# A diffusion layer on one core: the late modulation vectors as row sums on VectorE instead of products over partitions

## The chip, the cores and the metric

One core of one Trainium2 chip runs the whole kernel. The metric is device time in microseconds of one execution; the median of three timed runs of the kernel before is 1482.44 us (1481.68 to 1483.52). Engines are named TensorE (PE in the rows), VectorE (DVE), ScalarE (ACT) and GpSimd (POOL); transfers are issued from the queues of SyncE (SP) and GpSimd.

## The reference, cut to what matters

One layer of a diffusion backbone runs on 256 tokens and a context of 256 tokens, all in fp32. Six modulation vectors of 2048 features come from one product of the silu of the condition vector with a 2048 x 12288 matrix; everything else is large matrix products, a state space mixer (S5), a convolution and an attention of four heads.

```python
def _adaln(c_vec, w_mod, b_mod):
    m = jax.nn.silu(c_vec) @ w_mod + b_mod
    return jnp.split(m[..., None, :], 6, axis=-1)
...
sh1_x, sc1_x, g1_x, sh2_x, sc2_x, g2_x = _adaln(c, w_mod[l], b_mod[l])
...
hx = _rmsnorm(x, norm1_g[l]) * (1.0 + sc1_x) + sh1_x
zx = hx @ w_in[l] + b_in[l]
...
x = x + g1_x * (jnp.concatenate([s5_x, cv_x, ml_x], axis=-1) @ w_out[l])
hx2 = _rmsnorm(x, norm2_g[l]) * (1.0 + sc2_x) + sh2_x
x = x + g2_x * _swiglu(hx2, w_ffn_in[l], w_ffn_out[l])
```

The first two vectors (shift and scale of the first norm) are needed at the start. The other four, here called the late modulations and numbered q = 0 to 3 (g1, sh2, sc2, g2), are needed from the output projection on: q = 0 there, q = 1 and 2 at the second norm, q = 3 where the feed-forward output is added.

## The kernel before, in words

Features lie on partitions and tokens along the row. Every large weight matrix is cut into 128 x 128 tiles; they stream in one fixed order, eight tiles (512 KB) to a weight group, 386 groups in all. For each group SyncE loads `raw`, ScalarE casts it to `whi` (L201), and VectorE forms the rest `wlo = raw - whi` (L168). Each tile is then used by three matmuls (`mm3`): high x high, high x low, low x high. `raw`, `whi` and `wlo` have three buffers each, so VectorE can be ahead of TensorE by no more than that. The groups of the stages are: 0 to 13 phase 1, 14 to 29 the convolution's columns, 30 to 39 keys, 40 to 55 values, 56 to 71 queries, 72 to 87 the output gate o, 88 and 89 the S5 gate (glu), 90 to 121 the output projection in two halves, 122 to 385 the feed-forward.

Beside this main stream run side jobs, which are generators: the S5 mixer (16 pairs, each a chain between VectorE, ScalarE and TensorE), the convolution, the gates, the four attention heads, and the late modulations (`mod_job`). The class `Sched` keeps rough costs of the engines; at each weight group `pump` lets ready jobs emit steps, by priority, as long as the costs of VectorE and ScalarE are not too far ahead of TensorE. `need_mod(q)` forces the job on where a late modulation must be there. After that the compiler's list order fixes the sequence on every engine, and at run time each engine works through its own sequence.

A late modulation is a 2048 x 2048 product with a vector. It is taken in four blocks b of 512 output features. Weights come in slabs of 128 x 1024 (512 KB, tile `wm`, four buffers, issued from GpSimd's queue, L331); a slab holds 2 row tiles of 512 output features. Input features lie on partitions. For q = 0 (the set `MOD_PE`) TensorE multiplies: 16 native fp32 matmuls of 128x512 per block, four at a time on the 32-column strips of the array (L208, `ps_b<-wm,cs`). For q = 1 to 3 VectorE accumulates `macc = w * s + macc`, 15 instructions of 128x512 per block after one on ScalarE; each reads the result of the one in front. In both cases the sum over partitions is still to be taken: TensorE transposes `macc` (L749, four per block), and ScalarE sums the rows with an accumulating activation (L755), or VectorE reduces. `GO_AT` and `phase` hold q = 1 and 2 back until the keys, and q = 3 until the feed-forward has begun.

Of the kernel before, what the change touches and what calls it, by code (L numbers as in the profile page):

```python
# [19 lines left out]
KT = 16  # L20
# [14 lines left out]
MOD_PACE = 3200.0  # L35
MOD_PACE_F = 4000.0
MOD_PACE_D = 5000.0
# [6 lines left out]
GO_AT = {'k': 2}  # L44
LEAD_R, LEAD_S = 2, 1
MOD_PE = {(0, b) for b in range(4)}


# [58 lines left out]
class Sched:  # L107
    """Emits the tensor engine's main work in order and slips steps of side jobs in between."""
# [42 lines left out]
def hybrid_layer_kernel(ctx: ExitStack, tc: tile.TileContext, xt, ctxt, wm1, wmr, wst, wg, bvrow, pvd, cstd, s5p, out):  # L151
# [197 lines left out]
    # the order of the loads that share the queue up to the end of phase 1: by when they are needed  # L349
# [20 lines left out]
    cs = sb.tile([128, KT, 32], F32, name="cs")  # L370
# [3 lines left out]
    b1sc = sb.tile([128, 16], F32, name="b1sc")  # L374
# [66 lines left out]
    def s5_params():  # L441
# [43 lines left out]
        # half-angle sine and cosine  # L485
# [17 lines left out]
        # lambda_bar - 1 and its quotient by lambda  # L503
# [15 lines left out]
        # powers of lambda_bar  # L519
# [126 lines left out]
    def fourA(n, src, ps):  # L646
        """column tiles in turn, each over all rows: x tokens only"""
# [9 lines left out]
    def conv_job():  # L657
# [14 lines left out]
        def sum4(x):  # L672
            """sums over partitions and the four tiles, every partition the same"""
# [36 lines left out]
    def phase(n):  # L710
        mst["go"] = max(mst["go"], GO_AT.get(n, 0))

# [6 lines left out]
    def mod_job():  # L719
      for q in range(4):  # L720
        while mst["go"] < q:
            yield 500
        for b in range(4):
            on_pe = (q, b) in MOD_PE
            acc = sb.tile([128, 512], F32, name="macc", tag="macc", bufs=1)
            if on_pe:
                psm = bbank()
            for kp in range(0, 8, 2):
                w = [wm.pop((q, b, kp + i)).rearrange("p (k n) -> p k n", k=2) for i in range(2)]
                for j in range(4):  # L730
                    kt = 2 * kp + j
                    wj = w[j // 2][:, j % 2, :]
                    s = cs[:, kt, 0:1]
                    if on_pe:
# [675 lines left out]
```

## Time and profile before

| | |
|---|---|
| median of 3 timed runs | 1482.44 us |
| span of the profiled execution | 1479.6 us |
| TensorE busy | 1437.5 us, 97% |
| TensorE weight loads busy | 1351.2 us, 91% |
| VectorE busy | 1005.1 us, 68% |
| ScalarE busy | 716.0 us, 48% |
| DMA | 315.56 MB, 213 GB/s in the mean |

The profiled execution is not one of the three timed ones. Its span, from the first to the last instruction, is 2.84 us under their median; those 2.84 us are taken as what lies around the span. Busy shares of a whole span mix stages. In the slices of 37 us VectorE stands at 8 or 9 tenths busy from 160 to 440 us and at 4 or 5 tenths in the last third. A busy TensorE is modelled from pipelined matmuls, so a slice at 9 tenths can still hold short waits. The granted TensorE clock is 0.989 of full speed in the mean.

### The profile page before, as it was taken

The page shows a single profiled execution, that of the slowest core. Times are in us where ns is not written, and L with a number is a line of the kernel's source. Part 1 is how long each engine was busy: PE and PEld are TensorE (multiplying, and loading weights), DVE is VectorE, ACT ScalarE, POOL GpSimd, SP SyncE. Part 2 cuts the span into 40 slices and gives each one's busy share as a digit, 9 for nine tenths or more (in the row PEclk, how much of TensorE's full clock was granted, in tenths as well). Part 3 has the DMA queues.
Part 4 walks back from the last instruction along what each step waited for, and adds up shares of the span by engine and source line. Part 5 has one row for each costly group of instructions (what it writes and reads, how often), then busy time and mean ns, then how long its engine had stood idle before and what let it go on. Part 6 is the DMA issues. An engine that isn't in the chain of part 4 may idle for free.

```text
span 1479.6 us, 29243 instructions
## 1 busy us (share of the span) xinstructions
PE 1437.5 (97%) x11840; PEld 1351.2 (91%) x11840; DVE 1005.1 (68%) x1960; ACT 716.0 (48%) x1199; POOL 107.2 (7%) x207
## 2 busy tenths in 40 slices
PE   5999899999999999999899999999999999999996
PEld 3888788887888999999899999999999999999996
DVE  7555699988978887888776677455454554455554
ACT  4334776653565555645544444433444334443353
POOL 1221111110101110011000010000000000000000
PEclk9999999999999999999999999999999999999998
DMA  9997464442526666789477787555565555555553
GB/s 360 368 354 291 160 219 136 162 163 86 169 88 228 214 217 227 268 304 353 143 234 265 282 299 239 183 185 186 183 185 185 188 189 181 188 185 186 185 177 114
DMA packets 87943, 315.56 MB, mean 213 GB/s; under 512 B 10096, under 2 KB 10880, under 8 KB 87808
## 3 DMA queue, kind: packets, MB, share of 16 engines
q1 hardware_dynamic: 60912, 216.67, 44.1%
q0 software_dynamic: 26896, 97.02, 18.4%
q8 instruction: 93, 1.52, 0.4%
q14 instruction: 42, 0.34, 0.1%
HBM read 311.55 MB, written 2.10 MB: 212 GB/s over the span
## 4 chain that ended last, share of the span: by engine, by line
PE 89%; DVE 5%; ACT 3%; DMA 1%; issue 1%; SPq 0%; DVEq 0%; ACTq 0%
PE ps_m L208 70%; PE ps_b L208 13%; PE ps_qk L208 5%; DVE tmp L168 1%; DMA tmp<-in_wg_dram 1%; ACT tmp L195 0%; DMA raw<-in_wst_dram 0%; PE ps_b L839 0%; ACT whi L201 0%; ACT U L201 0%; DVE wlo L168 0%; DMA xr<-in_xt_dram 0%; ACT gT L201 0%; PE ps_b L749 0%; DVE tmp L191 0%
## 5 line engine op out<-in xcount | busy, mean ns | idle before, releaser
L168 DVE TENSOR_TENSOR wlo<-raw,whi 128x1024 fp32r<-128x1024 f32 x386 | 471.6, 1223 | 317.7 <-ACT whi L201 309.5
L201 ACT CAST whi<-raw 128x1024 fp32r<-128x1024 f32 x386 | 404.0, 1047 | 508.6 <-PE ps_m L208 373.8
L208 PE MATMUL ps_m<-h,whi 128*128 128x256 f32 x2624 | 470.4, 282 | 3.6 <-ACT h L195 3.6
L208 PEld LDWEIGHTS ps_m<-h,whi 128*128 128x128 f32 x2624 | 404.1, 189 | 4.0 <-ACT h L195 4.0
L208 PE MATMUL ps_m<-h,wlo 128*128 128x256 f32 x1312 | 370.0, 282 | 0.0
L208 PE MATMUL ps_m<-ffa,whi 128*128 128x256 f32 x1408 | 251.0, 281 | 0.0
L208 PEld LDWEIGHTS ps_m<-h,wlo 128*128 128x128 f32 x1312 | 247.8, 189 | 0.0
L208 PEld LDWEIGHTS ps_m<-ffa,whi 128*128 128x128 f32 x1408 | 215.7, 188 | 1.4 <-issue 1.2
L208 PE MATMUL ps_m<-ffa,wlo 128*128 128x256 f32 x704 | 197.2, 280 | 0.0
L208 PE MATMUL ps_m<-hx,whi 128*128 128x256 f32 x960 | 186.8, 290 | 5.5 <-ACT hx L195 3.6
L208 PEld LDWEIGHTS ps_m<-hx,whi 128*128 128x128 f32 x960 | 148.8, 190 | 24.8 <-issue 16.3
L179 DVE SCALAR_TENSOR_TENSOR macc<-wm,cs,macc 128x512 f32<-128x512 f32 x180 | 134.3, 746 | 6.6 <-ACT macc L195 5.1
L208 PE MATMUL ps_m<-hx,wlo 128*128 128x256 f32 x480 | 135.9, 284 | 0.0
L208 PEld LDWEIGHTS ps_m<-ffa,wlo 128*128 128x128 f32 x704 | 132.2, 188 | 0.0
L331 POOL DMA_DIRECT2D wm<-in_wmr_dram x128 | 67.5, 528 | 614.6 <-DVE macc L179 432.9
L208 PEld LDWEIGHTS ps_m<-hx,wlo 128*128 128x128 f32 x480 | 90.9, 190 | 0.2 <-DVE wlo L168 0.2
L179 DVE SCALAR_TENSOR_TENSOR xres<-ps_m,mods,xres 128x256 f32<-128x256 f32 x96 | 46.1, 481 | 35.0 <-PE ps_m L208 34.8
L179 DVE SCALAR_TENSOR_TENSOR XB<-XB,pv 128x256 f32<-128x256 f32 x120 | 53.7, 479 | 0.6
L208 PE MATMUL ps_m<-hc,whi 128*128 128x256 f32 x256 | 52.0, 284 | 0.0
L208 PE MATMUL ps_m<-mixm,whi 128*128 128x256 f32 x256 | 47.3, 286 | 0.0
L208 PE MATMUL ps_m<-whi,hx 128*128 128x512 f32 x128 | 46.5, 400 | 0.0
L201 ACT CAST ffa<-tmp 128x256 fp32r<-128x256 f32 x44 | 17.7, 405 | 49.6 <-DVE tmp L168 49.6
(267 smaller groups left out, 1997.3 us busy)
## 6 DMA issues: line engine op xcount, KB each, us to landing
raw<-in_wst_dram SPq DMA_DIRECT2D x386, 512.0 KB, 4.1
wm<-in_wmr_dram POOLq DMA_DIRECT2D x128, 512.0 KB, 5.2
wm<-in_wm_dram POOLq DMA_DIRECT2D x32, 512.0 KB, 7.2
wmu<-in_wm_dram POOLq DMA_DIRECT2D x16, 512.0 KB, 7.0
wmt<-in_wm_dram POOLq DMA_DIRECT2D x7, 512.0 KB, 6.4
wm<-in_wm_dram SPq DMA_DIRECT2D x5, 512.0 KB, 10.5
xr<-in_xt_dram SPq DMA_DIRECT2D x4, 512.0 KB, 6.6
cr<-in_ctxt_dram SPq DMA_DIRECT2D x4, 512.0 KB, 9.8
```

What stands on the lines that cost most here:

```text
L168: V.tensor_tensor(out=o, in0=a, in1=b, op=op)
L179: V.scalar_tensor_tensor(o, a, s, b, op0=op0, op1=op1)
L201: S.copy(o, a)
L208: i = P.matmul(o, lhsT=l, rhs=r, start=start, stop=stop, skip_group_check=sgc, **kw)
L331: i = (q or nc.gpsimd).dma_start(wm[key], src)
```

## The change

The weight of a late modulation is stored the other way round: output features on partitions, input features along the row. A slab is now (q, i, hf): 128 output features of column tile i, and the half hf of 1024 input features. A row of 1024 values of c is spread to all 128 partitions (`cbr`) and passed through silu on ScalarE. One VectorE instruction then multiplies slab and row and sums along the row into one column of `mods` or of `mpart`. There are 128 such instructions of 128x1024, one per slab. The sums of both halves are added at the end of each q. The matmuls, transposes and accumulating activations of the late modulations are gone, and so are the holds of `GO_AT`. `cbr` is loaded three times, since it takes the one buffer of `cs`: the first half for q = 0 to 2, the second half for q = 0 to 3, the first half again for q = 3.

```diff
-MOD_PACE = 3200.0
-MOD_PACE_F = 4000.0
-MOD_PACE_D = 5000.0
+MOD_PACE = (8000.0, 5000.0, 4000.0)
...
-GO_AT = {'k': 2}
...
-MOD_PE = {(0, b) for b in range(4)}
...
-    def stt(o, a, s, b, op0, op1):
-        V.scalar_tensor_tensor(o, a, s, b, op0=op0, op1=op1)
+    def stt(o, a, s, b, op0, op1, accum=None):
+        V.scalar_tensor_tensor(o, a, s, b, op0=op0, op1=op1, accum_out=accum)
...
-    cs = sb.tile([128, KT, 32], F32, name="cs")
+    cs = sb.tile([128, KT, 32], F32, name="cs", tag="cs")
...
-    mq = [(q, b, kp) for q in range(4) for b in range(4) for kp in range(8)]
-    mst = {"d": 0, "q": 0, "go": 0}
+    mq = [(q, i, hf) for hf, qs in ((0, (0, 1, 2)), (1, (0, 1, 2, 3)), (0, (3,))) for q in qs for i in range(KT)]
+    mst = {"d": 0, "q": 0}
...
-                    if on_pe:
-                        mm(psm[32 * j:32 * j + 32, :], cs[:, kt, :], wj, kt < 4, kt >= 12, native=True, tp=(0, 32 * j),
-                           pin=j > 0)
-                    elif kt == 0:
-                        act(acc, wj, AF.Copy, scale=s, pin=q == 3)
-                    else:
-                        stt(acc, wj, s, acc, OP.mult, OP.add)
...
-            for j in range(4):
-                P.transpose(ps[:, 128 * j:128 * j + 128], acc[:, 128 * j:128 * j + 128], ident)
-                sc.pe += 110
...
+        at, cbr, part = None, None, None
+        for n, (q, i, hf) in enumerate(mq):
+            if hf != at:
+                at, cbr = hf, sb.tile([128, 1024], F32, name="cbr", tag="cs")
+                nc.gpsimd.dma_start(cbr, crow[0:1, 1024 * hf:1024 * hf + 1024].to_broadcast([128, 1024]))
+                yield 4000
+                act(cbr, cbr, AF.Silu)
+                yield 2000
+            second = hf == (q < 3)
+            if second and i == 0:
+                part = sb.tile([128, KT], F32, name="mpart", tag="b1sc")
+            w = wm.pop((q, i, hf))
+            stt(w, w, 1.0, cbr, OP.mult, OP.mult, part[:, i:i + 1] if second else mods[:, q, i:i + 1])
+            mod_dma()
+            if second and i == KT - 1:
+                tt(part, part, pvc("bm", 32 + 16 * q, KT), OP.add)
+                tt(mods[:, q], mods[:, q], part, OP.add)
+                mst["q"] = q + 1
+            yield MOD_PACE[0 if n < 16 else 1 if n < 96 else 2]
...
-    phase("k")
...
-            mst["go"] = 3
...
-    mr = wmod[:, 4096:].reshape(8, 2, 128, 4, 4, 512)
-    a["wmr"] = np.ascontiguousarray(mr.transpose(3, 4, 0, 2, 1, 5)).reshape(4, 4, 8, 128, 1024)
+    a["wmr"] = np.ascontiguousarray(wmod[:, 4096:].T.reshape(4, KT, 128, 2, 1024).transpose(0, 1, 3, 2, 4))
+    a["crow"] = np.ascontiguousarray(f["c"][0:1])
```

The order of the side jobs shifts with it. Three places show how.

TensorE, at the glu stage (`gs` is the S5 output, `vx` the values of the attention, L1144 and L1110 the transposes that read a finished head). Before:

```order
L208 MATMUL ps_m<-gs,whi 128x256 x2
L208 MATMUL ps_m<-gs,wlo 128x256
L1144 MATMUL ps_b<-cst,RH 128x128 x6
L208 MATMUL ps_m<-gs,whi 128x256 x2
L208 MATMUL ps_m<-gs,wlo 128x256
```

After:

```order
L204 MATMUL ps_m<-gs,whi 128x256 x2
L204 MATMUL ps_b<-vx,RH 128x257 x7
L204 MATMUL ps_b<-negM,idr 128x256 x2
L204 MATMUL ps_m<-gs,wlo 128x256
```

The products of the fourth head with its values stood ten weight groups earlier, in the o stage; now they stand inside glu, and S5, whose last pair stood at group 55, ends at group 70.

VectorE, between the low halves of weight groups 91 and 93, where the output projection begins. Before:

```order
L168 TENSOR_TENSOR wlo<-raw,whi 128x1024
L179 SCALAR_TENSOR_TENSOR macc<-wm,cs,macc 128x512
L168 TENSOR_TENSOR tmp<-gT,tmp 128x256
L168 TENSOR_TENSOR wlo<-raw,whi 128x1024
L168 TENSOR_TENSOR mixs<-tmp,mixs 128x256
L168 TENSOR_TENSOR tmp<-gT,tmp 128x256
L168 TENSOR_TENSOR wlo<-raw,whi 128x1024
```

After, a part of what stands between two low halves (`qh`, `mvv` and `RH` belong to the fourth head):

```order
L175 SCALAR_TENSOR_TENSOR wm,mpart<-wm,cbr 128x1024
L1073 BN_AGGR mvv<-st_6735 128x2
L175 SCALAR_TENSOR_TENSOR wm,mpart<-wm,cbr 128x1024
L175 SCALAR_TENSOR_TENSOR tmp<-tmp 128x2
L175 SCALAR_TENSOR_TENSOR wm,mpart<-wm,cbr 128x1024
L175 SCALAR_TENSOR_TENSOR tmp<-mvv,tmp 128x2
L175 SCALAR_TENSOR_TENSOR wm,mpart<-wm,cbr 128x1024
L175 SCALAR_TENSOR_TENSOR tmp<-tmp 128x2
L175 SCALAR_TENSOR_TENSOR wm,mpart<-wm,cbr 128x1024
L171 TENSOR_SCALAR RH<-qh,mvv,tmp 128x256 x2
L164 TENSOR_TENSOR tmp<-gT,tmp 128x256
```

Between these two low halves there are 12 of the new instructions, woven into the end of the fourth head. One new instruction is written `wm,mpart<-wm,cbr` or `wm,mods<-wm,cbr`.

VectorE, at the second norm, from the first step of the inverse root (`rs`) to the first scaled tile. Before:

```order
L179 SCALAR_TENSOR_TENSOR tmp<-tmp 128x256
L179 SCALAR_TENSOR_TENSOR tmp<-ps_qk,tmp 128x256
L179 SCALAR_TENSOR_TENSOR rs_8355<-tmp 128x256
L168 TENSOR_TENSOR tmp<-xres,rs_8355 128x256
L175 TENSOR_SCALAR tmp<-tmp,A_7792,mods 128x256
```

After:

```order
L175 SCALAR_TENSOR_TENSOR tmp<-tmp 128x256
L175 SCALAR_TENSOR_TENSOR wm,mpart<-wm,cbr 128x1024
L175 SCALAR_TENSOR_TENSOR tmp<-ps_qk,tmp 128x256
L175 SCALAR_TENSOR_TENSOR wm,mpart<-wm,cbr 128x1024
L175 SCALAR_TENSOR_TENSOR rs_8146<-tmp 128x256
L175 SCALAR_TENSOR_TENSOR wm,mpart<-wm,cbr 128x1024
L164 TENSOR_TENSOR tmp<-xres,rs_8146 128x256
L175 SCALAR_TENSOR_TENSOR wm,mpart<-wm,cbr 128x1024
L171 TENSOR_SCALAR tmp<-tmp,A_7583,mods 128x256
```

Four new instructions stand inside that chain.

## Rows read from the trace of the kernel before

In each window the number in brackets behind a busy time counts instructions; behind the engines stand the granted clock, the DMA share and GB/s.

**Rows 1.** Windows by stage: start:end, length, busy us of PE, PEld, DVE, ACT, POOL.

```profile
134.10:220.30 86.20, 81.02 (x710) 70.96 (x700) 65.11 (x166) 63.05 (x114) 9.53 (x18) 0.96 0.57 199
220.30:321.60 101.30, 99.74 (x915) 85.34 (x914) 93.30 (x263) 62.32 (x144) 12.66 (x24) 1.00 0.44 147
321.60:450.90 129.30, 129.02 (x824) 105.56 (x824) 107.78 (x276) 66.72 (x152) 9.57 (x18) 1.00 0.38 125
450.90:591.80 140.90, 139.19 (x967) 129.89 (x966) 115.00 (x264) 80.48 (x157) 13.72 (x26) 0.99 0.67 224
591.80:615.20 23.40, 21.33 (x173) 20.28 (x172) 20.05 (x39) 17.69 (x35) 1.58 (x3) 1.00 0.65 244
615.20:697.50 82.30, 82.30 (x697) 80.54 (x697) 74.44 (x105) 38.13 (x62) 12.14 (x23) 1.00 0.92 326
697.50:757.00 59.50, 55.00 (x439) 54.09 (x438) 41.23 (x77) 31.92 (x51) 0.53 (x1) 0.94 0.53 171
```

**Rows 2.** Chain of waits, 930 to 1440 us: start, length, what (instructions).

```profile
940.30 480.32 PE ps_m L208 x4053
```

**Rows 3.** Groups by line and shape: count, busy us, mean ns, then idle before.

```profile
L179 DVE SCALAR_TENSOR_TENSOR macc<-wm,cs,macc 128x512 f32<-128x512 f32 x180 | 134.3, 746 | 6.6 <-ACT macc L195 5.1
L179 DVE SCALAR_TENSOR_TENSOR XB<-XB,pv 128x256 f32<-128x256 f32 x120 | 53.7, 479 | 0.6
L208 PE MATMUL ps_b<-wm,cs 128*32 128x512 f32 x128 | 20.0, 612 | 0.0
L168 DVE TENSOR_TENSOR tmp<-LC,cc 128x160 f32<-128x160 f32 x64 | 17.7, 317 | 0.2 <-ACT Wb L201 0.2
L168 DVE TENSOR_TENSOR tmp<-LW,bb 128x128 f32<-128x128 f32 x64 | 14.5, 281 | 0.0
```

**Rows 4.** Windows of the instructions on `macc` alone (PE: its transposes).

```profile
134.10:450.90 316.80, 3.17 (x20) 2.19 (x20) 15.66 (x21) 4.90 (x14) 0.99 0.45 152
450.90:591.80 140.90, 1.80 (x12) 1.46 (x12) 35.81 (x49) 5.58 (x27) 0.99 0.67 224
591.80:615.20 23.40, 0.60 (x4) 0.46 (x4) 4.40 (x6) 1.45 (x9) 1.00 0.65 244
615.20:697.50 82.30, 1.20 (x8) 0.93 (x8) 32.78 (x45) 4.15 (x19) 1.00 0.92 326
697.50:1479.60 782.10, 2.99 (x20) 2.34 (x20) 45.62 (x61) 8.54 (x44) 0.99 0.61 199
```

**Rows 5.** Timeline of VectorE, 582 to 586 us: start, length, instruction.

```profile
582.02 1.22 DVE L168 TENSOR_TENSOR wlo<-raw,whi 128x1024 fp32r<-128x1024 f32 x1
583.16 2.32 DVE L179 SCALAR_TENSOR_TENSOR macc<-wm,cs,macc 128x512 f32<-128x512 f32 x3
585.40 1.22 DVE L168 TENSOR_TENSOR wlo<-raw,whi 128x1024 fp32r<-128x1024 f32 x1
```

**Rows 6.** Timeline of ScalarE, 440 to 441 us.

```profile
440.63 0.19 ACT L755 ACTIVATION_READ_ACCUMULATOR macc<-ps_b 128x1 f32 x1
440.73 0.27 ACT L755 ACTIVATE macc<-ps_b 128x128 f32<-128x128 f32 x1
...
440.97 0.28 ACT L755 ACTIVATE macc<-ps_b 128x128 f32<-128x128 f32 x1
```

**Rows 7.** Window of the instructions on the S5 tile `Vr` alone (VectorE).

```profile
134.10:450.90 316.80, 59.59 (x144) 0.99 0.45 152
```

**Rows 8.** Timeline of VectorE, the fourth head, 555 to 577 us.

```profile
555.61 0.87 DVE L168 TENSOR_TENSOR qh<-ps_qk,cst 128x128 f32<-128x128 f32 x4
...
576.32 0.74 DVE L175 TENSOR_SCALAR RH<-qh,mvv,tmp 128x256 f32<-128x256 f32 x2
```

**Rows 9.** Timeline of VectorE at the second norm.

```profile
705.28 0.42 DVE L179 SCALAR_TENSOR_TENSOR tmp<-tmp 128x256 f32<-128x256 f32 x1 [0.81 <-ACT tmp L195]
...
707.26 0.41 DVE L175 TENSOR_SCALAR tmp<-tmp,A,mods 128x256 f32<-128x256 f32 x1
```

**Rows 10.** DMA issues by line: count, size of one, median us to landing.

```profile
wm<-in_wmr_dram POOLq DMA_DIRECT2D x128, 512.0 KB, 5.2
```

More of the change, by code (lines that the diff above doesn't have):

```diff
@@ L150, in hybrid_layer_kernel @@
 @with_exitstack
-def hybrid_layer_kernel(ctx: ExitStack, tc: tile.TileContext, xt, ctxt, wm1, wmr, wst, wg, bvrow, pvd, cstd, s5p, out):
+def hybrid_layer_kernel(ctx: ExitStack, tc: tile.TileContext, xt, ctxt, wm1, wmr, wst, wg, bvrow, crow, pvd, cstd, s5p, out):
     nc = tc.nc
@@ L373, in hybrid_layer_kernel @@
     act(cs[:, :, 1], pvc("cc", 0, 16), AF.Silu)
-    b1sc = sb.tile([128, 16], F32, name="b1sc")
+    b1sc = sb.tile([128, 16], F32, name="b1sc", tag="b1sc")
     ts(b1sc, pvc("bm", 16, 16), 1.0, OP.add)
@@ L705, in hybrid_layer_kernel @@
     mods = sb.tile([128, 4, 16], F32, name="mods")
-    mq = [(q, b, kp) for q in range(4) for b in range(4) for kp in range(8)]
-    mst = {"d": 0, "q": 0, "go": 0}
-    def phase(n):
-        mst["go"] = max(mst["go"], GO_AT.get(n, 0))
+    mq = [(q, i, hf) for hf, qs in ((0, (0, 1, 2)), (1, (0, 1, 2, 3)), (0, (3,))) for q in qs for i in range(KT)]
+    mst = {"d": 0, "q": 0}
     def mod_dma():
@@ L719, in mod_job @@
     def mod_job():
[L720 to L725, printed above, removed]
-            if on_pe:
-                psm = bbank()
-            for kp in range(0, 8, 2):
-                w = [wm.pop((q, b, kp + i)).rearrange("p (k n) -> p k n", k=2) for i in range(2)]
-                for j in range(4):
[L731 to L734, printed above, removed]
-                        mm(psm[32 * j:32 * j + 32, :], cs[:, kt, :], wj, kt < 4, kt >= 12, native=True, tp=(0, 32 * j),
-                           pin=j > 0)
-                    elif kt == 0:
-                        act(acc, wj, AF.Copy, scale=s, pin=q == 3)
-                    else:
-                        stt(acc, wj, s, acc, OP.mult, OP.add)
-                mod_dma()
-                mod_dma()
-                yield 2 * (MOD_PACE if on_pe else MOD_PACE_D if q < 3 else MOD_PACE_F)
-            dst = mods[:, q, 4 * b:4 * b + 4]
-            if on_pe:
-                acopy(acc, psm)
-            ps = bbank()
-            for j in range(4):
-                P.transpose(ps[:, 128 * j:128 * j + 128], acc[:, 128 * j:128 * j + 128], ident)
-                sc.pe += 110
-            if on_pe:
-                rsum(dst, ps.rearrange("p (f j r) -> p f j r", f=4, j=4)[:, :, :, 0])
-            else:
-                for j in range(4):
-                    S.activation(acc[:, 128 * j:128 * j + 128], ps[:, 128 * j:128 * j + 128], AF.Copy,
-                                    accum_out=dst[:, j:j + 1])
-                    sc.act += 390
-            tt(dst, dst, pvc("bm", 32 + 16 * q + 4 * b, 4), OP.add)
-            yield
-        mst["q"] = q + 1
@@ L762, in need_mod @@
     def need_mod(q):
-        mst["go"] = max(mst["go"], q)
         while mst["q"] <= q:
@@ L928, in hybrid_layer_kernel @@
     s5j = sc.add(s5_job(), P_S5)
-    phase("conv2")
     cdone = set()
@@ L1010, in hybrid_layer_kernel @@
         k_out(ct, ps)
-    phase("v")
     sc.finish(cvj)
@@ L1122, in hybrid_layer_kernel @@
     aj = sc.add(attention(), P_ATT)
-    phase("q")
     for ct in range(8):
@@ L1385, in pack @@
     return a
-_INS = ["xt", "ctxt", "wm1", "wmr", "wst", "wg", "bvrow", "pvd", "cstd", "s5p"]
+_INS = ["xt", "ctxt", "wm1", "wmr", "wst", "wg", "bvrow", "crow", "pvd", "cstd", "s5p"]
 def kernel(**inputs):
```

1 line of the change is left out of this document (removed).

## The prediction

> **What bounds the kernel now.** I read the windows by stage first, then the chain of waits, then the groups by line, and last the timelines at the places that the new order touches. The windows [rows 1] show TensorE busy nearly all the time in every stage, and VectorE next to it: 93.3 of 101.3 us in the keys, 107.8 of 129.3 in the values, 115.0 of 140.9 in queries and o, 74.4 of 82.3 in the output projection. So from 134 to 697 us two engines stand close to full, and neither can be given work freely. Behind 757 us it is different: 480.3 us of the chain of waits is one piece of TensorE, 4053 matmuls at 118.5 ns [rows 2], and VectorE stands at 4 or 5 tenths in the slices of the page. The late modulations cost TensorE 20.0 us of matmuls [rows 3] and 9.8 us of transposes (the sum of the windows of `macc`), and VectorE 134.3 us in 180 instructions of 746 ns [rows 3, 4]. Of these 134 us, 88.7 lie before 697 us and 45.6 behind it, where VectorE has room.
>
> **The price of one new instruction.** No row shows it. The old form of two SBUF operands takes 479 ns for 256 columns and 746 for 512 [rows 3], 267 ns for 256 more, so 1024 columns come to 746 + 534 = 1280 ns. In a row of unlike instructions the next one starts before the last has ended: `wlo`, 1.22 us long, is followed after 1.14 us, while three dependent `macc` steps take 2.24 us, 0.75 each [rows 5]. The new ones do not depend on each other, so 1.20 us from start to start is the low end. They also write out a sum. On ScalarE that is a second instruction: the read of the accumulator lasts 0.19 us and the next activation starts 0.10 us behind it [rows 6]. With 0.10 I take 1.30 us; the high end is 1.28 + 0.19, about 1.47. For 128 slabs that is 166 us (154 to 188) against 134 before: VectorE gets some 32 us more in all, TensorE loses some 30.
>
> The Trainium skill (VectorE: DVE Perf Modes, section on two Vector instructions with no wait between them) says that a Vector instruction that also writes out its accumulator is two instructions. ScalarE's rows show that form for its own sums, and no row here shows it for VectorE; without the second instruction the sum below would be 0.10 us less per slab, 13 us in all and some 6 to 8 on the path.
>
> **Where the work goes, stage by stage.** The order of the changed program was counted: 40 of the 128 new instructions stand before the low half of weight group 56, 30 in queries and o, 18 from glu to group 93, 28 in the rest of the output projection, 12 at the second norm and the head of the feed-forward, none behind group 135. All of VectorE's 45.6 us from behind 697 us thus move to the front, all but a part of the 12.
>
> - *Convolution, keys, values (134.1 to 450.9 us, 316.8 long).* TensorE is relieved of the 20.0 us of matmuls and 3.2 us of transposes [rows 3, 4]. VectorE loses 15.7 us of `macc` and gains 40 x 1.30 = 52 us. Since it is pushed, the scheduler lets 5 of the 16 S5 pairs slip behind group 55. A pair costs VectorE at least (59.6 + 17.7 + 14.5) / 16 = 5.7 us [rows 3, 7], so 28.7 us leave. From 266.2 us [rows 1] VectorE comes to 273.8: nearly as loaded as before, but TensorE has 23 us less and five pairs less. If VectorE's chains set this stretch nothing is won; if VectorE never idles, 43 us are won. I take TensorE's own relief, 23 us, since both engines were about equally near their limit: **-23** (-43 to 0).
> - *Queries and o (450.9 to 591.8, 140.9 long).* VectorE: 115.0 - 35.8 + 28.7 (the five pairs) + 39.0 = 146.9 us in a stretch of 140.9 [rows 1, 4], less what the fourth head takes away by slipping to glu. TensorE gets the five pairs' products too. **+6** (0 to +16).
> - *Glu and the first tiles of the output projection (591.8 to 615.2, 23.4 long).* VectorE: 20.05 - 4.40 + 18 x 1.30 = 39.1 us, and the tail of the fourth head, for which I put 8 us: the head lasts from 555.61 to 577.06 [rows 8], and about a third of that is work of its own. That makes 47 us where 23.4 were. TensorE has no other work left to hide it, since the o columns are done and the output projection waits behind glu in the same order. **+24** (+14 where the head runs earlier than its place says, +36 where its chain of 21 us is stretched by the instructions woven in).
> - *Rest of the output projection (615.2 to 697.5).* VectorE: 74.44 - 32.78 + 36.4 = 78.1 us, still under 82.3. Slabs: 28 where some 24 were, at 326 GB/s and 0.92 DMA share [rows 1], 4 x 0.524 MB = 6.4 us of transfer if nothing hides it; 1.2 us of transposes go. **+2** (-1 to +6).
> - *Second norm.* Four new instructions stand inside the chain that TensorE waits for, from 705.28 to 707.26 [rows 9]: 4 x 1.30 = 5.2 us with nothing over them. The other eight go into VectorE's idle time (41.2 of 59.5 us busy [rows 1]). **+5** (+2 to +9).
> - *Feed-forward.* 3.0 us of transposes go from a stretch that TensorE alone sets [rows 2, 4]; what leaves VectorE there is worth nothing. **-3** (-4 to -1).
>
> What leaves ScalarE (the accumulating activations and copies on `macc`) is off the path in all stages. GpSimd's queue holds slabs, the S5 inputs and `cbr` in one order; a slab that waits for its buffer holds the S5 input behind it, which is in the bounds of the first two terms.
>
> The sum is -23 + 6 + 24 + 2 + 5 - 3 = +11 us against the profiled span: 1479.6 + 11 = 1490.6, and with 2.8 us around it **1493.4 us**. The sum of the low ends is -32, of the high ends +66.
>
> **The rivals.** *A, faster: the front stretch gives more than the late head costs.* If VectorE closes its 43 us of idle time in the S5 stretch, queries and o stay as long as they were, and glu costs only the 14 us: -43 + 0 + 14 + 2 + 5 - 3 = -25, 1457 us. For it: TensorE was modelled busy 309.8 of 316.8 us there, so its relief could be worth more than its own 23 us once the pairs slip. Against it: in the keys VectorE is at 92% already, and a chain that passes through three engines leaves gaps. With the other terms as forecast it decides once the first term passes -34.
>
> *B, slower than forecast: the new instructions wait for data at the head of VectorE's queue.* A slab takes 5.2 us to land [rows 10] and there are four buffers: 5.2 + 1.3 = 6.5 us for four, 1.63 us per instruction in a burst. For the 18 at glu that is 0.33 x 18 = +6. The spread row `cbr` has one buffer and is reloaded twice, each time behind the last use: 5.2 us to land if it is like a slab, then the silu behind what stands in ScalarE's queue, which I put at 2 us; VectorE's queue stands for these 7 us if the next product has been reached. +14. Together 1513 us. Behind a standing product there is always a `wlo`, for which TensorE waits. Against it: the order leaves three to four weight groups between the two.
>
> *C, a sum costs a second pass.* An accumulating instruction with two SBUF operands that ran at half speed would take 1.07 us more, 2.37 us: VectorE would be over its stage everywhere (term one 0, queries and o +38, glu +43, output projection 74.44 - 32.78 + 66.4 - 82.3 = +26, norm +9, -3), +113, 1595 us. The rows without a sum give 1.04 ns per column [rows 3], no sign of halving; none shows one with a sum. The Trainium skill (Vector Engine (DVE) Microarchitecture Reference, section 7, points that are easy to get wrong) says that this form with two non-bf16 SBUF sources halves throughput, as no port is left for the accumulator. The rows without a sum do not agree with it.
>
> That the change does not do what it says is no rival: in the order every matmul on `cs` and every transpose of `macc` is gone.
>
> **How the numbers follow.** Forecast 0.55 (own range 1478 to 1510), A 0.25, B 0.16, C 0.04. A measurement of this kernel can tell about 0.2% from no change, 1479.5 to 1485.4. Faster: nine tenths of A and a little of the forecast, 0.25. Same: the rest of A and a tenth of the forecast, 0.09. Slower: 0.66. The range leaves out the far half of A and C: 1463 to 1528.
>
> **What would show it.** Right: windows by stage with the stretch up to values some 23 us shorter, glu and the first tiles twice as long with VectorE full, and four products in the norm's chain before the first scaled tile; one product with its read at 1.3 us from start to start. Wrong: TensorE idle in the keys as long as before (the first term falls), or a fourth head that is done before glu (the third falls). VectorE standing in front of a product with a DMA as releaser would speak for B, a product of over 2 us for C.

## Result and the profile after

The changed kernel takes 1497.47 us (median of 4 runs, 1495.83 to 1499.85) against 1482.06 us: a ratio of 1.0107, 95% interval 1.0092 to 1.0121. It is slower, as forecast, and 4 us above the forecast of 1493.4. Its profiled execution spans 1495.6 us, 16.0 more than before.

The windows by stage of the kernel after answer to [rows 1] (start:end, length, busy us of PE, PEld, DVE, ACT, POOL, then granted clock, DMA share, GB/s). From top to bottom they are the convolution, keys, values, queries, o, glu with the first output tiles, the rest of the output projection, and the second norm. They are cut where the low half (`wlo`) of weight groups 14, 30, 40, 56, 72, 88, 94, 122 and 138 is done.

```profile
133.80:211.40 77.60, 67.62 (x579) 65.36 (x571) 67.30 (x148) 54.03 (x84) 10.10 (x19) 0.93 0.67 234
211.40:291.90 80.50, 77.34 (x704) 74.27 (x703) 76.19 (x203) 45.07 (x100) 2.14 (x4) 0.98 0.23 74
291.90:416.20 124.30, 123.06 (x753) 100.86 (x752) 114.81 (x279) 57.90 (x129) 16.96 (x32) 1.00 0.55 187
416.20:488.00 71.80, 70.47 (x649) 66.59 (x648) 65.26 (x165) 45.70 (x103) 4.82 (x9) 1.00 0.48 157
488.00:574.50 86.50, 79.51 (x512) 72.56 (x511) 73.51 (x189) 50.79 (x93) 13.18 (x25) 0.96 0.73 246
574.50:623.30 48.80, 34.94 (x209) 30.76 (x208) 43.68 (x110) 25.84 (x42) 9.50 (x18) 0.86 0.86 311
623.30:710.30 87.00, 84.50 (x715) 82.36 (x714) 80.09 (x128) 39.59 (x51) 15.31 (x29) 1.00 0.91 333
710.30:770.40 60.10, 50.31 (x389) 49.16 (x388) 50.71 (x96) 26.95 (x36) 4.22 (x8) 0.89 0.67 234
```

Before, the same cuts lie at 134.1, 220.3, 321.6, 450.9, 520.4, 591.8, 616.4, 697.5 and 752.4 us. The feed-forward is counted to the low half of the last group, at 1460.0 us before and 1476.0 after. Subtracting the lengths gives the terms of the sum:

| stage | before | after | difference | predicted |
|---|---|---|---|---|
| convolution, keys, values | 316.8 | 282.4 | -34.4 | -23 (-43 to 0) |
| queries and o | 140.9 | 158.3 | +17.4 | +6 (0 to +16) |
| glu, first output tiles | 24.6 | 48.8 | +24.2 | +24 (+14 to +36) |
| rest of the output projection | 81.1 | 87.0 | +5.9 | +2 (-1 to +6) |
| second norm | 54.9 | 60.1 | +5.2 | +5 (+2 to +9) |
| feed-forward | 707.6 | 705.6 | -2.0 | -3 (-4 to -1) |

With -0.3 us ahead of the convolution this is +16. The largest single loss is in glu: VectorE is busy 43.7 of 48.8 us there, TensorE 34.9, and TensorE's granted clock falls to 0.86.

The new instruction stands in two groups (line, engine, operation, tiles, shape, count, busy us, mean ns, idle before and what ended it):

```profile
L175 DVE SCALAR_TENSOR_TENSOR wm<-wm,cbr 128x1024 f32<-128x1024 f32 x128 | 154.8, 1220 | 7.8 <-DMA wm<-in_wmr_dram 4.9 <-ACT cbr L191 2.7
L175 DVE DVE_READ_ACCUMULATOR wm<-wm,cbr 128x1 f32 x128 | 10.9, 85 | 0.0
```

and so on VectorE's timeline (start, length), ahead of the second norm:

```profile
707.97 1.22 DVE L175 SCALAR_TENSOR_TENSOR wm<-wm,cbr 128x1024 f32<-128x1024 f32 x1
709.11 0.09 DVE L175 DVE_READ_ACCUMULATOR wm<-wm,cbr 128x1 f32 x1
709.11 1.22 DVE L164 TENSOR_TENSOR wlo<-raw,whi 128x1024 fp32r<-128x1024 f32 x1
710.25 1.22 DVE L175 SCALAR_TENSOR_TENSOR wm<-wm,cbr 128x1024 f32<-128x1024 f32 x1
```

The sum is read by a second instruction of 85 ns, but the next instruction starts in the same moment as the read: 1.14 us from a product to what follows. In all, VectorE stood idle for 7.8 us in front of products, 4.9 of them for slabs and 2.7 for `cbr`.

The S5 tile `Vr` counts the pairs, 9 instructions each (answers to [rows 7]; the last window is queries and o):

```profile
133.80:211.40 77.60, 6.56 (x16) 0.93 0.67 234
211.40:291.90 80.50, 15.83 (x38) 0.98 0.23 74
291.90:416.20 124.30, 19.04 (x45) 1.00 0.55 187
416.20:574.50 158.30, 18.51 (x45) 0.98 0.62 206
```

99 instead of 144 before the end of the values: five pairs moved into queries and o. In the keys 38 stand where 54 stood before.

The five pairs are work of TensorE, too. Its instructions on the S5 tile `Mb`, first up to the end of the values before and after, then in queries and o after (before, there are none):

```profile
134.10:450.90 316.80, 46.07 (x640) 0.99 0.45 152
133.80:416.20 282.40, 31.35 (x440) 0.98 0.49 168
416.20:574.50 158.30, 14.66 (x200) 0.98 0.62 206
```

and the same for the tile `U`:

```profile
134.10:450.90 316.80, 24.52 (x160) 0.99 0.45 152
133.80:416.20 282.40, 16.37 (x110) 0.98 0.49 168
416.20:574.50 158.30, 7.73 (x50) 0.98 0.62 206
```

So 22.9 us of TensorE's work left the front with the pairs, about as much as the modulation's own, and 22.4 us came back in queries and o. TensorE's busy time up to the end of the values fell from 309.8 to 268.0 us.

### The profile page after: what moved, and what is told of

The parts are those of the page before. It is cut to its first block, busy times and chain, and to the rows that moved or that the text cites. A ratio compares the mean times of both kernels' runs of the same rounds, so it can differ in the third digit from the quotient of the medians.

```text
span 1495.6 us, 28725 instructions
## 1 busy us (share of the span) xinstructions
PE 1420.9 (95%) x11648; PEld 1349.6 (90%) x11648; DVE 1022.6 (68%) x2024; ACT 698.9 (47%) x1092; POOL 109.0 (7%) x210
## 4 chain that ended last, share of the span: by engine, by line
PE 72%; issue 15%; DVE 5%; DMA 3%; POOL 3%; ACT 2%; SPq 0%; POOLq 0%; DVEq 0%; ACTq 0%
PE ps_m L204 59%; PE ps_b L204 9%; PE ps_qk L204 3%; POOL wm L327 3%; DMA wm<-in_wmr_dram 1%; DMA wm<-in_wm_dram 1%; DVE tmp L164 1%; DVE wlo L164 1%; DVE wm L175 1%; DMA tmp<-in_wg_dram 1%; DVE Vr L164 1%; PE ps_b L810 0%; DVE Vr L187 0%; DVE tmp L187 0%; ACT U L197 0%
## 5 line engine op out<-in xcount | busy, mean ns | idle before, releaser
L175 DVE SCALAR_TENSOR_TENSOR wm<-wm,cbr 128x1024 f32<-128x1024 f32 x128 | 154.8, 1220 | 7.8 <-DMA wm<-in_wmr_dram 4.9
L175 DVE SCALAR_TENSOR_TENSOR xres<-ps_m,mods,xres 128x256 f32<-128x256 f32 x96 | 46.2, 482 | 34.4 <-PE ps_m L204 34.2
## 6 DMA issues: line engine op xcount, KB each, us to landing
wm<-in_wm_dram SPq DMA_DIRECT2D x5, 512.0 KB, 10.7
```

Of the source, the lines that this page charges most:

```text
L175: V.scalar_tensor_tensor(o, a, s, b, op0=op0, op1=op1, accum_out=accum)
```

## The experiments

The theory at first ("theory 1") was that VectorE's total work between values and second norm sets the time. Stage lengths below are cut as above; every ratio is against the kernel before, run beside.

**The late end.** Two runs hold products of the last modulation back until the head of the feed-forward. `pin` keeps an instruction in the written order; both runs differ in one number (116 and 96):

```diff
+            while n >= 116 and mst["go"] < 3:
+                yield 500
...
-            stt(w, w, 1.0, cbr, OP.mult, OP.mult, part[:, i:i + 1] if second else mods[:, q, i:i + 1])
+            stt(w, w, 1.0, cbr, OP.mult, OP.mult, part[:, i:i + 1] if second else mods[:, q, i:i + 1],
+                pin=n >= 116)
...
+            mst["go"] = 3
```

> The changed kernel with its last 12 products, those at the second norm and the head of the feed-forward, tied behind group 166, where VectorE has room; the order up to group 122 is the same. Theory 1 (a product inside a chain that TensorE waits for costs its own length): the stretch of groups 122 to 138 falls from 60.1 us by 4 x 1.22 = 5 us to about 55, and the kernel comes to 1492 us. Rival (the stretch is long for another reason, such as the lower granted clock of 0.89 there or the second norm's inputs coming late): it stays within 1 us of 60.1 and the kernel within 1 us of 1497.

> The changed kernel with all 32 products of the last vector (q = 3) tied behind the head of the feed-forward, as the kernel before held them; up to group 101 the order is the same. Theory 1: the norm's stretch falls by 5 us as in the run with 12, the output projection, groups 94 to 122, which has 8 products in place of 28, falls from 87.0 us to the 81 to 82 of the kernel before, and the feed-forward does not grow: 1486 to 1487 us. Rival (the output projection is long because of the slabs and weights in transfer or of the late readout, not of VectorE's work): it stays at 85 to 87, 1491 us.

The first took 1489.1 us (1.0045, 1.0029 to 1.0062), the second 1487.7 (1.0030, 1.0014 to 1.0046). The windows of the norm in the first and of the rest of the output projection in the second:

```profile
707.50:760.10 52.60, 48.10 (x386) 47.27 (x385) 37.70 (x69) 26.84 (x36) 0.00 (x0) 0.97 0.56 186
```

```profile
622.10:705.50 83.40, 83.40 (x708) 81.62 (x708) 59.33 (x86) 37.34 (x49) 4.22 (x8) 1.00 0.68 233
```

Without the twelve products the norm falls from 60.1 to 52.6 us: the fifth term had its place and, at +5, about its size. With all 32 behind, the output projection gets only 3.6 us back although VectorE has 20.8 us less to do: TensorE is now busy for all of its 83.4 us, so that less work for VectorE could win no more there.

**Glu cleared.** On top of the second run, products 70 to 95 are released one per output tile instead of around glu, and the call that forces the second and third modulation moves from the middle of the output projection to near its end (not shown):

```diff
+            while 70 <= n < 96 and not mst.get("ok"):
+                yield 500
...
+        if ct >= 3:
+            mst["ok"] = 1
+            sc.step(mj)
+            mst["ok"] = 0
...
```

> As the run with q = 3 behind the head of the feed-forward, and in addition the 18 products between groups 88 and 94 are spread over the output projection, which then has 25; the fourth attention head is as late as in the changed kernel. Theory 1 (the products' own VectorE time makes glu and the first output tiles long): the stretch of groups 88 to 94 falls from 48.8 us by 18 x 1.22 = 22 to about 27, the output projection is at 84 to 87; kernel 1468 to 1472 us. Rival (the late fourth head's chain sets that stretch, and the products only fill its gaps): the stretch stays at 40 us or more, and the kernel at 1485 us or above.

1484.5 us (1.0012, 0.9998 to 1.0026). Glu, then the rest of the output projection:

```profile
573.20:610.90 37.70, 31.79 (x211) 28.99 (x210) 24.92 (x71) 25.26 (x42) 0.00 (x0) 0.91 0.45 154
610.90:706.40 95.50, 91.28 (x741) 87.52 (x739) 78.86 (x121) 39.87 (x52) 13.19 (x25) 0.98 0.81 284
```

This lies between the two expectations. Without one product glu still lasts 37.7 us against 24.6 before: 13 us of the third term are left to the fourth attention head that slipped into it (at a granted clock of 0.91), and 11 went with the 18 products and their slabs. The output projection takes 12 us more than in the run with the fourth modulation late, and the norm 4 less. Time moved rather than went.

**Lowest priority.** `P_MOD` from 2 to 5, nothing else:

```diff
-P_CONV, P_S5, P_MOD, P_ATT, P_GATE = (3, 3, 2, 4, 1)
+P_CONV, P_S5, P_MOD, P_ATT, P_GATE = (3, 3, 5, 4, 1)
```

> The changed kernel with the modulation job behind S5 and attention in the priority of the side jobs (5 in place of 2), nothing else. In its order the fourth head ends at group 80 in place of 89 and S5 at 62 in place of 70, 7 products in place of 18 stand between groups 88 and 94, 16 at the second norm. Theory 1 with the order as cause of the displaced head: groups 72 to 88 fall from 86.5 to about 73 us, groups 88 to 94 from 48.8 to about 28, the front (14 to 56) gives back some 5 to 10, the norm stays at 60: kernel 1468 to 1475 us, faster than the kernel before. Rival (VectorE is simply full, so work that is moved out of one stretch lengthens another by the same): the kernel stays at 1490 to 1500 us.

1509.8 us (1.0172, 1.0139 to 1.0205). Second half of the values, queries, glu:

```profile
354.60:435.40 80.80, 72.58 (x458) 58.93 (x457) 73.56 (x196) 44.16 (x104) 12.73 (x24) 0.96 0.57 196
435.40:524.10 88.70, 81.66 (x617) 74.19 (x616) 76.62 (x199) 54.53 (x115) 8.46 (x16) 0.98 0.54 178
598.10:622.80 24.70, 20.55 (x154) 19.74 (x153) 20.65 (x37) 14.51 (x20) 3.69 (x7) 0.93 0.85 324
```

Glu is as short as before, with the heads back in their places, and the whole is 12 us slower than the changed kernel, beyond both expectations. In the values VectorE is busy 73.6 of 80.8 us and TensorE waits; in the changed kernel that half took 71 with VectorE at 64.8. Here too the stage that is freed shifts its work into its neighbours.

**Half the product.** Each product over 512 of its 1024 columns:

```diff
-            stt(w, w, 1.0, cbr, OP.mult, OP.mult, part[:, i:i + 1] if second else mods[:, q, i:i + 1])
+            stt(w[:, 0:512], w[:, 0:512], 1.0, cbr[:, 0:512], OP.mult, OP.mult, part[:, i:i + 1] if second else mods[:, q, i:i + 1])
```

> The changed kernel with each product over 512 of its 1024 columns (the other half of each row sum is left out). All slabs are still loaded; TensorE does the same. A product should fall from 1.22 us to about 0.64 (0.53 by the two-operand rows of the kernel before, 746 ns for 512 columns, less the overlap, plus the read), 128 of them save VectorE some 70 to 80 us, all of it before 760 us. Theory 1 (VectorE's work between the keys and the second norm sets the time): some two thirds of it comes back on the path, queries and o, glu and the second norm shrink, 1497 goes to 1435 to 1460. Rival (the chains and the arrival of slabs set it, VectorE's length matters little): 1480 to 1495, with VectorE idle where it was busy.

1501.6 us (1.0129, 1.0111 to 1.0147): not even the rival allowed for that. The group of the halved products, and the window of o:

```profile
L175 DVE SCALAR_TENSOR_TENSOR wm<-wm,cbr 128x512 f32<-128x512 f32 x128 | 86.4, 687 | 39.3 <-DMA wm<-in_wmr_dram 34.9 <-ACT cbr L191 4.0
```

```profile
528.00:612.40 84.40, 75.15 (x504) 68.49 (x503) 62.56 (x190) 38.94 (x63) 20.60 (x39) 0.96 0.94 354
```

The products are 68 us shorter, and 39.3 us of idle time stand ahead of them, 34.9 ended by slabs. The scheduler, taking them for cheap, placed 66 instead of 30 in queries and o; their slabs filled the DMA engines to 0.94 in o. Glu (25.3 us) and the output projection (81.5) were as before the change, queries and o together 188.6 us instead of 158.3. This is rival B of the prediction, in a kernel that provokes it. Theory 1 in its plain form fell here: 68 us less of VectorE's work bought nothing. Why the queries alone grew to 104.2 us, with 3.8 us of waiting for slabs, was not settled. In the four runs where the last S5 pair ends in groups 62 to 64 (this one, the two with the lowest priority and the one with TensorE's work given back on the slabs) the queries last 87 to 104 us, in the others 70 to 78.

**Lowest priority and the last one late** (both edits above together):

> The changed kernel with the products at the lowest priority (as in the run with that one change) and, besides, the 32 products of the fourth modulation tied behind the head of the feed-forward. The order has 12 products fewer in the second half of the output projection and at the norm than that run. Theory 1 (VectorE's work before the norm sets the time, wherever it stands): 12 x 1.22 = 15 us of work leave, the output projection and the norm together come back by 12 to 17 us, 1510 goes to 1493 to 1498. Rival (what cost there was the order of the S5 pairs and the attention heads): within 5 us of that run, 1505 to 1515.

1523.5 us (1.0278, 1.0262 to 1.0294). Output projection and norm lasted 144.7 us against 157.1 in the run with the lowest priority alone: the 12 us that were expected. The loss was a fault of the edit, in the feed-forward, which grew by 25 us. At the lowest priority the fourth modulation was left until its result was needed at once, and TensorE stood 18.4 us in one piece (what waits, for what, us in total, times, longest):

```profile
PE ps_m L206 <- DVE xres L175: 18.4, 1, 18.4
```

**TensorE's work given back, on the slabs.** With each slab of the first modulation two matmuls of its old shape, with every eighth slab four transposes, results unused:

```diff
+                    mm(psm[32 * jj:32 * jj + 32, :], cbr[:, 0:32], w[:, 512 * j:512 * j + 512], True, True, native=True,
+                       tp=(0, 32 * jj), pin=jj > 0)
...
+                    P.transpose(pst[:, 128 * j:128 * j + 128], w[:, 128 * j:128 * j + 128], ident)
```

> The changed kernel with TensorE's work of the kernel before given back: 64 matmuls of 128x32 on 128x512 over the slabs of the first modulation and 64 transposes of 128x128, their results unused. VectorE's work is that of the changed kernel. By the rows of before this is 64 x 0.61 us at the most in one column group, about 10 us in the matmuls' own time with four groups side by side, and some 9 us of transposes. Theory 1 (VectorE sets the time between the values and the norm, TensorE sets the keys): +5 to +15 us against the changed kernel, most of it up to the values, none in glu. Rival A (TensorE's relief is what was won in front, all of it): the whole stretch up to the values goes back by 20 us or more, 1517 or above. Rival B (TensorE's relief was worth nothing, the gain came from VectorE's order): within 3 us, 1494 to 1500.

1561.1 us (1.0534). This says nothing on the question: the output projection alone grew by 50 us. It held 52 products instead of 29, and there TensorE stood 15 us in front of slabs and products 12 us in front of TensorE's work. A later run asks it again without such ties.

**A hybrid.** The first modulation stays on TensorE as before (32 slabs), the second and third are 64 products, the fourth's 32 come behind the head of the feed-forward:

```diff
+    m0 = [(0, b, kp, 0) for b in range(4) for kp in range(8)]
+    mp = [(q, i, hf) for hf, qs in ((0, (1, 2)), (1, (1, 2, 3)), (0, (3,))) for q in qs for i in range(KT)]
...
+            while n >= 64 and mst["go"] < 3:
+                yield 500
```

> A hybrid: the first modulation stays on TensorE as in the kernel before (32 slabs, 128 matmuls, 16 transposes), the second and third are 64 products, and the fourth's 32 products are tied behind the head of the feed-forward. VectorE has 64 x 1.22 = 78 us of modulation work before the second norm (before: 88.7 us, changed: 156); TensorE has 48 transposes less than before. Theory 1 (VectorE's work before the norm sets the time): faster than both, 1470 to 1478. Rival (the place of the work, not its sum: products among the S5 pairs, the heads and the values stretch them): 1480 to 1490, with values, queries and o longer than before.

1490.95 us (1.0056, 1.0038 to 1.0074). Values, queries, rest of the output projection:

```profile
318.20:459.30 141.10, 131.21 (x806) 106.72 (x805) 125.83 (x311) 64.40 (x143) 22.20 (x43) 0.95 0.60 208
459.30:534.50 75.20, 72.74 (x508) 66.39 (x507) 70.55 (x163) 44.84 (x83) 11.61 (x22) 0.98 0.74 251
628.30:708.20 79.90, 79.90 (x679) 78.17 (x678) 47.09 (x55) 34.31 (x43) 0.00 (x0) 1.00 0.58 190
```

Less work for VectorE ahead of the norm than in the kernel before, and slower: all 64 products stood in values, queries and o. The values grew by 12 us with VectorE at 125.8; the output projection, with 47.1 us of VectorE's work instead of 73.2 before between the same cuts, gained 1.2: TensorE is busy in all of it. The place counts, not only the sum.

**Without the slabs' transfers.** All but the first four slabs of the late modulations are not loaded, in the changed kernel's own order:

```diff
-        if mst["d"] < len(mq):
+        if mst["d"] < 4:
...
-            w = wm.pop((q, i, hf))
-            stt(w, w, 1.0, cbr, OP.mult, OP.mult, part[:, i:i + 1] if second else mods[:, q, i:i + 1])
+            w = wm[mq[n % 4]]
+            stt(w, w, 0.0, cbr, OP.mult, OP.mult, part[:, i:i + 1] if second else mods[:, q, i:i + 1])
```

> The changed kernel in the same order, with the late modulations' slabs left out but for the first four, which every product reads again (its factor is 0, so that it leaves zeros; the modulations come out as the biases alone). The products' count, form and places are those of the changed kernel; 124 transfers of 0.52 MB are gone. Theory 2 (VectorE's work sets glu and the first output tiles, and transfers are hidden): 1490 to 1498, the stretch of groups 88 to 94 at 45 us or more. Rival (transfers: 0.86 to 0.92 of the DMA engines were busy there): that stretch falls under 40 us, the output projection to 82, in all 1475 to 1485.

1485.2 us (1.0029, 1.0016 to 1.0042). Glu and the rest of the output projection:

```profile
568.80:614.80 46.00, 34.12 (x217) 30.38 (x216) 44.02 (x111) 25.72 (x42) 0.00 (x0) 0.89 0.31 104
614.80:697.30 82.50, 81.22 (x701) 79.27 (x700) 79.12 (x127) 39.79 (x52) 0.53 (x1) 1.00 0.58 192
```

Each of the two expectations holds in one place. Glu stays at 46 us: there VectorE's work and its chains set the length, the transfers 2.8 us of it. The output projection falls from 87.0 to 82.5 with VectorE as busy as in the changed kernel, so 4.5 us of it hang on the 28 slabs that were loaded there. By the medians 12 us of the changed kernel hang on 124 slabs (15 by the profiled executions). Not all of that is the change's: the kernel before loads the same slabs, but 28 of them behind the norm. Nor do transfers alone make the output projection long. In the kernel before it has nearly the same traffic, and TensorE is busy in all of it:

```profile
616.40:697.50 81.10, 81.10 (x687) 79.34 (x686) 73.24 (x103) 37.72 (x61) 12.14 (x23) 1.00 0.93 330
```

**What TensorE's relief is worth.** 64 matmuls of the old shape (128 records in the trace) and 16 transposes on a resident tile, without a reader, spread over convolution and keys; some reach into the values:

```diff
+                for j in range(4):
+                    mm(psm[32 * j:32 * j + 32, :], ident[:, 0:32], kT[:, 0, :], kp == 0, kp == 3, native=True,
+                       tp=(0, 32 * j), pin=j > 0)
```

> The changed kernel with 64 matmuls and 16 transposes of the first modulation's shapes put back on TensorE in the convolution and the keys, on a resident tile and without a reader, so that nothing waits for a slab (other than in the run before with TensorE's work given back). VectorE's work is that of the changed kernel, the order nearly too (four S5 pairs behind group 55 where five were, the products of the norm a little earlier). Theory 2 (TensorE's relief is what was won in front): convolution and keys, 158 us in the changed kernel and 187 before, come to 175 to 185, in all 1510 to 1518. Rival (the five displaced S5 pairs and VectorE's lighter load made the gain): 158 to 164 there, in all 1494 to 1500.

1500.9 us (1.0133, 1.0111 to 1.0155). The windows of convolution and keys, and the group of the spare matmuls in both:

```profile
133.90:211.20 77.30, 71.33 (x613) 62.43 (x602) 67.48 (x148) 53.09 (x83) 10.10 (x19) 0.98 0.67 236
211.20:304.20 93.00, 90.10 (x795) 78.97 (x794) 85.59 (x228) 47.75 (x105) 2.14 (x4) 0.98 0.19 64
```

```profile
L204 PE MATMUL ps_b<-kT,cst 128*32 128x512 f32 x104 | 18.3, 667 | 0.0
```

The S5 pairs stand stage by stage where they stand in after (16, 38, 45 and 45 instructions on `Vr`), so this is a clean comparison up to the values: the spare work, 18.3 us of matmuls here, cost 12.5 us in the keys, nothing in the convolution, and 10.7 us up to the end of the values (293.1 us against 282.4). It falls between the two expectations. In the convolution the granted clock rose with it from 0.93 to 0.98, and TensorE's busy time by only 3.7 us; what the work would have cost there at an equal clock is not shown. In the keys TensorE sets the length: 99.7 of 101.3 us busy before [rows 1], 77.3 of 80.5 after, 90.1 of 93.0 here. The relief is worth some 11 us of the 34 won in front. The other 24 are left to the five displaced pairs, with their 22.9 us of TensorE's work, and what moved along with them.

**The hybrid, spread.** The products of the hybrid take their factor from a column that a late result sets, so that none can run ahead (where it is set is not shown):

```diff
+    def allow(n, src):
+        mst["i"] = (mst.get("i", -1) + 1) % 8
+        one = ones8[:, mst["i"]:mst["i"] + 1]
+        ts(one, src, 0.0, OP.mult, 1.0, OP.add)
...
-            stt(w, w, 1.0, cbr, OP.mult, OP.mult, part[:, i:i + 1] if second else mods[:, q, i:i + 1],
+            stt(w, w, mst["one"], cbr, OP.mult, OP.mult, part[:, i:i + 1] if second else mods[:, q, i:i + 1])
```

> The hybrid again (first modulation on TensorE, 64 products for the second and third, the fourth behind the head of the feed-forward), with the products only moved: each takes its factor 1 from a column that a late result of TensorE sets, so that 6 stand in the first half of the values, 4 in the second, 8 in the queries, 15 in o, 31 from glu to the end of the output projection, none at the norm. The arithmetic and the sum of VectorE's work are those of the hybrid run (1491). Theory 2 (each stage has its own bound: TensorE from the values to the output projection as long as VectorE's work there stays under some nine tenths, VectorE beyond that): values back from 141 to about 128 us, queries from 75 to 69, output projection stays at 80 to 82, in all 1472 to 1480. Rival (it is the products' form, with its slabs of 1024 columns and their arrivals, that costs, wherever it stands): 1486 or above.

1500.1 us (1.0111, 1.0091 to 1.0131). Values, queries with o, rest of the output projection, first blocks of the feed-forward (groups 138 to 166); what VectorE waited for in queries and o; and the chain of waits in those blocks:

```profile
318.80:441.40 122.60, 122.31 (x783) 99.88 (x782) 99.50 (x257) 61.62 (x138) 10.02 (x19) 1.00 0.41 141
441.40:595.30 153.90, 149.71 (x1062) 138.16 (x1060) 118.49 (x291) 86.71 (x149) 12.68 (x24) 1.00 0.59 202
617.70:708.90 91.20, 83.62 (x666) 79.91 (x665) 78.04 (x123) 34.86 (x43) 14.78 (x28) 0.96 0.91 329
763.50:854.60 91.10, 85.73 (x696) 84.69 (x695) 76.25 (x111) 37.78 (x50) 15.30 (x29) 0.96 0.88 329
```

```profile
DVE ones L171 <- ACT RH L193: 9.1, 2, 6.4
```

```profile
795.37 7.37 DMA raw<-in_wst_dram
...
805.17 5.05 DMA raw<-in_wst_dram
...
811.38 8.39 DMA cbr<-in_crow_dram
```

The time lies where the rival put it, at 1486 or above. The values came back as theory 2 of this expectation says (122.6 instead of 141.1 us), and three other places gave it back: VectorE stood behind the releasing columns, 31 products stood from glu to the end of the output projection, and the first blocks of the feed-forward, a stretch where VectorE has room, held 31 products and lasted 9.7 us longer than in the kernel before. Two loads of weights stand in the chain of waits there, and a load of `cbr`; the median load of weights took 6.4 us to land, against 4.8 in the same groups before:

```profile
752.40:833.80 81.40, 81.23 (x685) 81.03 (x684) 61.41 (x79) 39.04 (x60) 8.44 (x16) 1.00 0.82 285
```

**The same, with the three mended:**

```diff
-        if ct in (0, 3, 6):
-            allow(4, qT[:, ct, 0:1])
+        if ct in (1, 4, 7):
+            allow(4, qT[:, ct - 1, 0:1])
...
+            if mst["go"] < 96:
+                allow(2, ffa[:, i - 1, 1, 0:1].bitcast(F32) if i else ffas[0][:, FBLK - 1, 1, 0:1].bitcast(F32))
```

> The spread hybrid with three things mended that its trace showed: the columns that release the products are set from results one column tile older (VectorE had stood 9 us in front of them in queries and o), 5 products fewer in the output projection and more in the values, and the 32 products behind the head of the feed-forward released two at a time over 16 blocks, where 30 of them had stood in the first 28 weight groups (91 us instead of 81, with the weights' own transfers late). Theory 2 (stage by stage bounds, transfers among them): first blocks of the feed-forward back to 81 to 82 us, output projection from 91 to 81 to 85, queries and o from 154 to 142 to 148, in all 1472 to 1482, at or under the kernel before. Rival (the products as such lengthen queries, o and the output projection, because VectorE delivers the split weights late behind instructions of 1.2 us): queries, o and the output projection stay within 3 us of that run, only the feed-forward comes back, 1486 to 1491.

1483.8 us (1.0017, 1.0005 to 1.0030), two us above the upper end of theory 2 and clear of the rival. Values, queries with o, rest of the output projection, first blocks of the feed-forward:

```profile
318.90:448.10 129.20, 129.01 (x842) 105.15 (x840) 109.24 (x280) 67.37 (x151) 12.66 (x24) 1.00 0.44 149
448.10:591.60 143.50, 142.03 (x989) 131.25 (x990) 114.98 (x276) 80.51 (x136) 12.70 (x24) 1.00 0.64 222
616.60:699.40 82.80, 80.88 (x668) 77.82 (x667) 72.12 (x112) 34.41 (x43) 12.17 (x23) 1.00 0.92 331
753.70:834.00 80.30, 80.30 (x679) 80.30 (x678) 59.03 (x83) 36.64 (x49) 7.42 (x14) 1.00 0.75 264
```

All three places came back, 16 us net with the same products. The values took 6.6 us, with five products more in them. TensorE is busy in nearly every microsecond of these stages, as in the kernel before, and the time is that kernel's to 0.2%. No version here beat it.

## Why the prediction was right, and where not

The direction and the size held, 16.0 us by the profile where +11 stood, and glu, the largest loss, came where it was put. Around the span lie 1.8 us in one and the same execution (1497.4 us against 1495.6), not the 2.8 that the forecast added.

*The price of a product* was 1.30 us in the sum and 1.14 to 1.22 on the chip. The estimate took ScalarE's 0.10 us for the read of the sum as an addition; on VectorE that read lies under the next instruction. The Trainium skill (VectorE: DVE Perf Modes, section on two Vector instructions with no wait between them) is right that there are two instructions: the trace has 128 reads of 85 ns. As a price the low end, 1.20, was the better choice. VectorE got some 20 us of work in all (154.8 against 134.3 of the products' own), not 32.

*Convolution, keys, values*, -34 where -23 stood. The step that failed is "I take TensorE's own relief, 23 us". The spare-work run puts that relief at 11. The remainder is left to the five pairs. That TensorE has "five pairs less" was said, but no time was put on it; the trace has 22.9 us of TensorE's work in them. The sign named against this term, TensorE idle in the keys as long as before, could not tell: it was idle there for 1.6 us before [rows 1] and for 3.2 after, while the keys lost 20.8. *Queries and o*, +17 where +6 stood and +16 was the end: the same five pairs coming back, priced there against VectorE's load but not against TensorE's (22.4 us) and the chain through three engines. Both errors are mostly one, and cancel: the two terms together came out at -17.0, as predicted. That agreement is luck: the sum was right there, not the working. In time, what the five pairs cost apart from the products that moved along with them was not separated.

*Glu*, +24 as predicted, by a different division, so that the exact number is luck, too: the fourth head 13 (I put 8), products 11 (I put 19, as 18 x 1.30 less the 4.4 of the old steps). That part of the products lies in gaps of the head's chain, which the sum did not grant, would explain it; no run shows it by itself.

*Rest of the output projection*, +5.9 at the upper end of +6. The bound there was the transfer of the four added slabs, 6.4 us. I took +2 on the belief that most of it would be hidden at a DMA share of 0.92. 4.5 us vanish when none of the 28 slabs is loaded; what the added ones cost is not shown. The part left with the fourth modulation late is work of TensorE, 83.4 us without a gap where 81.1 were.

*Second norm*, +5.2 for +5: with the twelve products held back 7.4 us left. *Feed-forward*, -2.0 for -3.

*The rivals.* A, faster, had -34 in the first term as its mark, and -34.4 came; but it also needed queries and o to stay as they were, and the pairs that made the front cheap made that stage dear. B had a real mechanism but not this place: VectorE stood 7.8 us in front of products in the changed kernel, and 39.3 us when they were halved. C fell with 1220 ns for 1024 columns, less than the 1280 that the form without a sum led to. The Trainium skill (Vector Engine (DVE) Microarchitecture Reference, section 7) has such an instruction at half throughput; the measurement decides against it.

## What to carry to other kernels

Where two engines are near full, price a move by stage: work put on the engine that sets a stage can cost its whole length (12.5 us for TensorE's spare work in the keys), work taken out where the other engine holds the bound returns almost nothing (1.2 us for 26 us of VectorE's in the output projection). When the scheduler shifts a dependent block across a stage border, book it as one sum over both stages, and on every engine that works for it; most of its gain in front came back as a loss behind here. Work moved to an idle engine brings its transfers along: ask of the queue and the memory, too, whether the new place has room.

## What was unexpected of the hardware

- The read of a Vector instruction's sum (85 ns) starts together with the instruction behind it and cost nothing in the queue: 1.14 us from a product to its successor, as behind a `wlo` without a sum [rows 5].
- With the factor in a column instead of a constant the same product took 1279 ns instead of 1220 (96 of them, in the spread hybrid); over 512 columns with a constant, 687 ns.
- 28 slabs and one `cbr` in 91 us of the feed-forward, at 329 GB/s and a DMA share of 0.88, went with a stretch 9.7 us longer; with 14 slabs in 80 us, at 264 GB/s, it was not. The rate alone is not the cause: at 330 GB/s and 0.93 TensorE had no gap in the output projection of the kernel before.
- In glu TensorE's granted clock was 0.86 with TensorE busy 34.9 of 48.8 us, where before it was 1.00 with 21.3 of 23.4 busy [rows 1]. The 0.86 is a mean of two levels: the clock was full (1.00, 2.4 GHz) from 590.5 to 602.0 us, where TensorE was busy for only 4.6 of 11.5 us, and half (0.50, 1.2 GHz) from 602.1 to 612.2. What part of the stretch is due to the clock alone was not separated.
